# Two attention score maps in one tile of two PSUM banks, the neighbourhood bias added by VectorE, and another order of the mixers' steps

## The chip, the cores and the metric

The kernel runs on one core of a Trainium2 chip. The metric is the time on the device, in microseconds (us), of one execution of the whole program. TensorE is called PE here, VectorE DVE, ScalarE ACT, GpSimd POOL, and SyncE, which issues most of the transfers, SP.

## What is computed

The reference runs 256 latent tokens of width 1024, with 256 context tokens beside them, through two blocks of two layers each. The change touches the first block alone, and of it the four mixers and the projection behind them. Cut to these:

```python
def first_block(...):                       # layers l = 0, 1
    mod = s_c @ ada_w[l] + ada_b[l]         # six vectors; the same for the context
    hx = rms_norm(x, norm1_g[l]) * (1.0 + sc1) + sh1
    y  = token_mixers(hx, hc, ...)          # below
    x  = x + g1 * y
    x  = x + g2 * expert_choice_ffn(...)    # router, 16 experts

def token_mixers(...):
    ya = chunk_spatial_gating(aX, ...)      # gating
    yb = fourier_mix(bX)                    # Fourier
    # C, differential attention: two maps per head
    s = einsum('bqhmd,bkhmd->bhmqk', q, k) * 32 ** -0.5
    a = softmax(s)
    w = a[:, :, 0] - lam * a[:, :, 1];  yc = w @ v
    # D, neighbourhood attention: bias on the local keys, then all keys
    s_loc = q @ k_blk * 64 ** -0.5 + bias
    p = softmax(concat(s_loc, s_ctx));  yd = p @ v
    # merge: every group normed per head of 64, then the output matrix
    y = rms_norm(concat(ya, yb, yc, yd)) * head_scale
    return y @ w_out
```

In layer 0 the context tokens pass the mixers too (4 tiles of 128 tokens, `nt` = 4), in layer 1 only the latent tokens do (`nt` = 2).

## The kernel before, in words

Each layer of the first block goes through the mixers and the projection (`mixers` L621, `project` L604 on), the router, and 16 experts with their weights streamed from HBM. The second block follows and is not touched.

**How the mixers are staged.** The normed input is transposed by PE (`hx` L286 to L301, tiles `pt`). Column blocks of the input matrix give queries, keys and values (products `pj`, three matmuls for each piece since the operands are split in a high and a low part, L316 to L318; the split of a weight tile is L62 on ACT and L63 on DVE). `diff_unit` (L438 to L468) is one unit of C, a tile of 128 queries and one head with its two maps. `na_unit` (L470 to L502) is one unit of D, a tile of queries and two heads. Layer 0 has 16 units of C and 8 of D, layer 1 has 8 and 4. In both, each of the two score maps has a PSUM tile `psc` of one bank. In a unit of D on latent queries (t < 2, four units in each layer) the bias is put into PSUM by a matmul with the identity (L484), the scores are added to it (L485), DVE takes the row maximum (L489) and negates it (L490), ACT takes the exponentials `e` (L494), PE transposes them into the same bank (L426), ACT copies them out as `wT` (L428), PE multiplies with the values into the same bank (L435), and DVE writes the scaled result to `y` (L502):

```python
nc.tensor.matmul(ps[:, 0:256], C.id, bias[:, i], start=True, stop=False, skip_group_check=True)
nc.tensor.matmul(ps[:, :n], self.dqT[r, j, ...], self.dkT[r, j, k0:k0 + n], start=(t >= 2), ...)
...
wT = self.weights_T(M, pss[i], es[i], n)
o = self.pv(pss[i], wT, n, self.dv, t0, h)
```

The bias tile of a unit has one buffer and comes from HBM by SP's queue (L476). Between these steps stand those of the modulation (`pada`, L182, with its own row `ab` loaded by POOL's queue, L171), of the Fourier part (`bz`, F) and of the gating (s).

**Norm and merge.** Each of the four results y0 (gating), y1 (Fourier), y2 (C), y3 (D) is squared on ACT (L558), summed on DVE (L559), scaled (L560), put through ten small DVE operations of an inverse root (L37 to L41) and multiplied on DVE (L366). `merge` (L575 to L588) transposes them on PE (tiles `pty`, one bank, L583), ACT and DVE write them out as `yT` (L587, L588). The first column block of the projection adds the groups up in the order `self.ks`.

**What sets the order.** `ORDER1` is a string for each layer that lists the steps: ck, cq, cv and dk, dq, dv are projections, C and D the attentions, aN stands for N modulation steps, oN for the norm of group N, r for the router. The order of the o entries is also `ks`. A list scheduler then places every instruction on its engine by data dependencies and estimated durations, so the strings give priorities and the final order is the scheduler's.

**PSUM.** The projections have two banks (`acc`), the scores and transposes four (`E.s`, pool `ps`, four buffers of one bank), `m` and `ada` one each.

Of the kernel before, what the change touches and what calls it, by code (L numbers as in the profile page):

```python
# [14 lines left out]
D = 1024  # L15
# [81 lines left out]
def load_consts0(E, pool):  # L97
# [11 lines left out]

ORDER1 = ("ck a3 cv cq C dk a3 a3 a2 dv a3 dq bz F a2 D s a3 o1 o2 a5 r o0 o3",  # L110
          "ck a4 a1 cv cq C dk a2 bz dv a3 dq s a1 F a5 D a6 o1 r o0 o2 o3")

# [91 lines left out]
class G1:  # L204
# [75 lines left out]
    def hx(self, M):  # L280
# [7 lines left out]
        for s in range(2):  # L288
# [3 lines left out]
            for k in range(0, KC, 2):  # L292
                pt = E.s.tile([128, 2, 256], FT, name="pt1", tag="s")
                for j in range(2):
# [144 lines left out]
    def diff_unit(self, M, t, h):  # L439
# [5 lines left out]
        rq = self.rq[:, 8 * t + 2 * h:8 * t + 2 * h + 2]  # L445
        pss, es = [], []
        for i in range(2):
            f = 64 * (h % 2) + 32 * i
            r = slice(f, f + 32)
            ps = E.s.tile([128, 512], FT, name="psc", tag="s")  # L450
            nc.tensor.matmul(ps[:, :n], self.cqT[r, h // 2, 128 * t:128 * t + 128], self.ckT[r, h // 2, k0:k0 + n], start=True, stop=True)  # L451
            pss.append(ps)
        for i in range(2):
            nc.vector.tensor_reduce(mx[:, i:i + 1], pss[i][:, :n], axis=AX.X, op=OP.max)
        nc.vector.scalar_tensor_tensor(mx, mx, -1.0, rq, op0=OP.mult, op1=OP.mult)
# [14 lines left out]
    def na_unit(self, M, t, j):  # L470
# [3 lines left out]
        if t < 2:  # L474
            bias = M.tile([128, 2, 256], FT, name="bias", tag="bias", bufs=1)
            nc.sync.dma_start(bias, E.i["na_bias"][self.l, :, t, 2 * j:2 * j + 2])  # L476
        sm = E.md.tile([128, 2], FT, name="smd", bufs=4)
        mx = E.md.tile([128, 2], FT, name="mxd", bufs=4)
        pss = []
        for i in range(2):  # L480
            r = slice(64 * i, 64 * i + 64)
            ps = E.s.tile([128, 512], FT, name="psc", tag="s")
            if t < 2:
                nc.tensor.matmul(ps[:, 0:256], C.id, bias[:, i], start=True, stop=False, skip_group_check=True)  # L484
            nc.tensor.matmul(ps[:, :n], self.dqT[r, j, 128 * t:128 * t + 128], self.dkT[r, j, k0:k0 + n],  # L485
                             start=(t >= 2), stop=True, skip_group_check=True)
            pss.append(ps)
        for i in range(2):
            nc.vector.tensor_reduce(mx[:, i:i + 1], pss[i][:, :n], axis=AX.X, op=OP.max)  # L489
        nc.vector.tensor_scalar(mx, mx, -1.0, None, op0=OP.mult)  # L490
# [82 lines left out]
    def merge(self):  # L573
# [4 lines left out]

        self.ks = [2 * int(st[1]) + j for st in ORDER1[self.l].split() if st[0] == "o" for j in range(2)]
        for k in self.ks:  # L580
            pt = E.s.tile([128, 512], FT, name="pty", tag="s")
            for t in range(nt):
                nc.tensor.transpose(pt[:, 128 * t:128 * t + 128], self.y[k // 2][:, t, 128 * (k % 2):128 * (k % 2) + 128], C.id)  # L583
            g = self.pc[:, 16 + k:17 + k]
            for s in range(nt // 2):
                p = pt[:, 256 * s:256 * s + 256]
                nc.scalar.activation(yT[2 * s][:, k], p, AF.Copy, scale=g)  # L587
                nc.vector.scalar_tensor_tensor(yT[2 * s + 1][:, k], p, g, yT[2 * s][:, k], op0=OP.mult, op1=OP.subtract)  # L588
# [32 lines left out]
    def mixers(self):  # L621
        E, l, mods = self.E, self.l, self.mods
        pool = E.tc.tile_pool
        with pool(name=f"mix{l}", bufs=1) as M, \
                pool(name=f"ps{l}", bufs=4, space=PSUM) as E.s, pool(name=f"pm{l}", bufs=1, space=PSUM) as E.m, \
                pool(name=f"pd{l}", bufs=1, space=PSUM) as E.ad:
# [1213 lines left out]
```

## Time and profile before

| what | value |
|---|---|
| median of 3 runs | 2824.7 us (2815.96 to 2825.24) |
| the profiled execution | 2826.67 us |
| its span in the trace | 2824.9 us |
| mean granted PE clock | 0.96 |
| busy: PE, weight loads, DVE, ACT, POOL | 2527.0, 1740.5, 1354.1, 818.2, 243.5 us |

By the names of the instructions in the timeline the span falls into these stages: start 0 to 45 us, mixers and projection of layer 0 to 345, router to 375, experts to 860, mixers and projection of layer 1 to 1045, router to 1075, experts to 1545, and the second block to 2825. A window's row gives the busy time of each engine in it, and the granted clock as a share of full speed; a matmul in fp32 appears as several records, whose pipelined ends overlap.

### The profile page before, as it was taken

The numbers are of one execution on the slowest core, as the hardware profiler recorded it, in microseconds if no ns is written. First come the engines' busy times: TensorE is split into PE (matmuls) and PEld (weight loads), VectorE is DVE, ScalarE is ACT, GpSimd is POOL, SyncE is SP. The second block draws the span as 40 slices with busy tenths as digits, with TensorE's granted clock in tenths as the row PEclk, the third lists the DMA queues.
The fourth block names the chain that finished last, engine by engine and source line by source line (L and its number), as shares of the span: only waits on it lengthen the run. The fifth ranks groups of instructions, "written<-read, shape, count | busy, mean of one in ns | idle before, by whom it ended". The sixth has DMA issues, their size and how long they took to land.

```text
span 2824.9 us, 42465 instructions
## 1 busy us (share of the span) xinstructions
PE 2527.0 (89%) x17771; PEld 1740.5 (62%) x17771; DVE 1354.1 (48%) x2663; ACT 818.2 (29%) x1339; POOL 243.5 (9%) x293
## 2 busy tenths in 40 slices
PE   6999989988889997666667999999999999999998
PEld 4776743322227662111114988888997888879996
DVE  4446533232236562001103768456656667556765
ACT  2334311000014430000002434334444433334442
POOL 1000110000000010000000122000202031100200
PEclk9999999999999999888899998999999998999999
DMA  7434469999995568999996421335654431325553
GB/s 292 180 120 147 164 272 421 422 421 421 421 381 181 185 242 360 422 421 421 421 421 264 155 91 53 113 111 175 209 181 138 152 118 46 105 90 194 179 192 121
DMA packets 237459, 665.60 MB, mean 236 GB/s; under 512 B 11572, under 2 KB 165860, under 8 KB 182356
## 3 DMA queue, kind: packets, MB, share of 16 engines
q1 hardware_dynamic: 235428, 657.81, 61.2%
q0 software_dynamic: 1696, 4.59, 0.5%
q8 instruction: 139, 2.28, 0.3%
q14 instruction: 52, 0.43, 0.0%
q10 hardware_dynamic: 144, 0.49, 0.0%
HBM read 661.78 MB, written 1.05 MB: 235 GB/s over the span
## 4 chain that ended last, share of the span: by engine, by line
PE 59%; DMA 24%; issue 9%; DVE 5%; POOL 2%; ACT 1%; SPq 0%; DVEq 0%; ACTq 0%; POOLq 0%
DMA w<-in_exp_w_up 8%; DMA w<-in_exp_w_down 8%; PE acc L84 6%; PE acc L86 6%; DMA w<-in_exp_w_gate 6%; PE acc L85 6%; PE pj L316 3%; PE pj L318 3%; PE pgate L862 3%; PE pj L317 3%; PE pd L862 2%; PE pup L862 2%; PE pada L182 2%; PE psc L435 1%; PE psc L451 1%
## 5 line engine op out<-in xcount | busy, mean ns | idle before, releaser
L63 DVE TENSOR_TENSOR whl<-w,whl 128x1024 fp32r<-128x1024 f32 x376 | 469.2, 1251 | 310.0 <-ACT whl L62 309.4
L62 ACT ACTIVATE whl<-w 128x1024 fp32r<-128x1024 f32 x376 | 396.2, 1058 | 472.3 <-PE acc L86 237.0
L84 PE MATMUL acc<-xh,whl 128*128 128x256 f32 x1664 | 476.5, 286 | 0.5 <-DVE xh L1619 0.5
L86 PE MATMUL acc<-xh,whl 128*128 128x256 f32 x1664 | 471.7, 283 | 0.2
L85 PE MATMUL acc<-xl,whl 128*128 128x256 f32 x1664 | 471.1, 283 | 0.0
L84 PEld LDWEIGHTS acc<-xh,whl 128*128 128x128 f32 x1664 | 316.7, 190 | 11.0 <-issue 6.5
L86 PEld LDWEIGHTS acc<-xh,whl 128*128 128x128 f32 x1664 | 316.4, 190 | 5.6 <-issue 3.6
L85 PEld LDWEIGHTS acc<-xl,whl 128*128 128x128 f32 x1664 | 316.8, 190 | 3.3 <-issue 2.5
L862 PE MATMUL pup<-w,xg 128*64 128x512 f32 (+1 forms) x1024 | 221.4, 662 | 67.9 <-DMA w<-in_exp_w_up 67.9
L862 PE MATMUL pgate<-w,xg 128*64 128x512 f32 (+1 forms) x1016 | 218.5, 648 | 45.8 <-DMA w<-in_exp_w_gate 43.4
L862 PE MATMUL pd<-w,ehT 128*64 128x512 f32 (+1 forms) x1024 | 202.7, 622 | 59.3 <-DMA w<-in_exp_w_down 42.3
L862 PEld LDWEIGHTS pup<-w,xg 128*64 128x64 f32 (+1 forms) x1024 | 52.6, 130 | 228.7 <-DMA w<-in_exp_w_up 149.6
L862 PEld LDWEIGHTS pd<-w,ehT 128*64 128x64 f32 (+1 forms) x1024 | 51.7, 125 | 186.5 <-DMA w<-in_exp_w_down 87.2
L862 PEld LDWEIGHTS pgate<-w,xg 128*64 128x64 f32 (+1 forms) x1016 | 50.9, 127 | 177.7 <-DMA w<-in_exp_w_gate 91.8
L316 PE MATMUL pj<-whl,hT 128*128 128x256 f32 x496 | 144.5, 292 | 6.1 <-ACT hT L300 5.8
L318 PE MATMUL pj<-whl,hT 128*128 128x256 f32 x496 | 143.3, 290 | 0.9 <-DVE hT L301 0.9
L317 PE MATMUL pj<-whl,hT 128*128 128x256 f32 x496 | 142.8, 289 | 0.0
L893 DVE TENSOR_TENSOR od<-pd,g 128x512 f32<-128x512 f32 x24 | 16.6, 691 | 232.0 <-PE pd L862 232.0
L881 DVE SCALAR_TENSOR_TENSOR et<-et,pup 128x512 f32<-128x512 f32 x24 | 16.5, 687 | 224.0 <-PE pup L862 223.8
L316 PEld LDWEIGHTS pj<-whl,hT 128*128 128x128 f32 x496 | 94.5, 191 | 24.7 <-issue 10.9
L317 PEld LDWEIGHTS pj<-whl,hT 128*128 128x128 f32 x496 | 94.5, 191 | 13.1 <-issue 8.9
L318 PEld LDWEIGHTS pj<-whl,hT 128*128 128x128 f32 x496 | 94.5, 191 | 8.5 <-issue 5.7
(607 smaller groups left out, 4158.9 us busy)
## 6 DMA issues: line engine op xcount, KB each, us to landing
w<-in_exp_w_down SPq DMA_DIRECT2D x128, 1024.0 KB, 19.8
w<-in_exp_w_up SPq DMA_DIRECT2D x127, 1024.0 KB, 19.8
w<-in_exp_w_gate SPq DMA_DIRECT2D x125, 1024.0 KB, 19.8
w<-in_w_in SPq DMA_DIRECT2D x82, 1024.0 KB, 5.1
w<-in_ada_w SPq DMA_DIRECT2D x48, 1024.0 KB, 6.4
w<-in_w_ffn_up SPq DMA_DIRECT2D x44, 1024.0 KB, 5.1
w<-in_w_ffn_down SPq DMA_DIRECT2D x22, 1024.0 KB, 4.8
w<-in_w_out SPq DMA_DIRECT2D x16, 1024.0 KB, 5.5
```

The lines of the kernel that those rows point to most:

```text
L62: nc.scalar.activation(h, w, AF.Copy)
L63: (engine or nc.vector).tensor_sub(lo, w, h)
L84: nc.tensor.matmul(ps[:, b], h[:, k], xh[:, k], start=(k == 0), stop=False)
L85: nc.tensor.matmul(ps[:, b], h[:, k], xl[:, k], start=False, stop=False)
L86: nc.tensor.matmul(ps[:, b], lo[:, k], xh[:, k], start=False, stop=(k == KC - 1))
L182: nc.tensor.matmul(self.ps[32 * j:32 * j + 32], self.st[:, k], ws[j], start=(k == 0), stop=(k == KC - 1), skip_group_check=True)
L316: nc.tensor.matmul(ps, xh, wh, start=start, stop=False, skip_group_check=bool(ks))
L317: nc.tensor.matmul(ps, xh, wl, start=False, stop=False, skip_group_check=bool(ks))
L318: nc.tensor.matmul(ps, xl, wh, start=False, stop=stop, skip_group_check=bool(ks))
L435: self.E.nc.tensor.matmul(o, wT[:, 128 * c:128 * c + 128], v[:, t0 + c, 64 * h:64 * h + 64], start=(c == 0), stop=(c == n // 128 - 1))
L451: nc.tensor.matmul(ps[:, :n], self.cqT[r, h // 2, 128 * t:128 * t + 128], self.ckT[r, h // 2, k0:k0 + n], start=True, stop=True)
L862: m = nc.tensor.matmul(ps[64 * h + mw * i:64 * h + mw * i + mw], lhs(kk, i, e), ws[i][k][:, 512 * h:512 * h + 512], start=(kk == 0), stop= ...
```

## The change

It does four things. (1) The two maps of a unit of C, and the two heads of a unit of D, get one tile `psc` of two banks in place of two tiles of one, and one reduction takes both row maxima. (2) The bias of D is no longer put into PSUM by matmuls with the identity; DVE adds it in place to the scores, one instruction of 128 partitions by 2 by 256 for each of the four latent units of a layer, and the bias tile is loaded by POOL's queue instead of SP's. (3) The transposes of `hx` and of `merge` use tiles of two banks, which hold four and two pieces, and the pool `E.s` has two buffers of two banks in place of four of one. (4) `ORDER1` puts D right behind C and its projections, ahead of Fourier and gating, spreads the modulation steps anew, and turns the o entries from 1, 2, 0, 3 (layer 0) and 1, 0, 2, 3 (layer 1) into 2, 3, 1, 0 in both.

```diff
@@ -107,8 +107,9 @@
 CAP = 32
 GELU_C = math.sqrt(2.0 / math.pi)
 
-ORDER1 = ("ck a3 cv cq C dk a3 a3 a2 dv a3 dq bz F a2 D s a3 o1 o2 a5 r o0 o3",
-          "ck a4 a1 cv cq C dk a2 bz dv a3 dq s a1 F a5 D a6 o1 r o0 o2 o3")
+
+ORDER1 = ("ck a3 cv cq C dk dv dq D a3 a3 a3 bz F a3 o2 s o3 o1 a4 a5 r o0",
+          "ck a4 a1 cv cq C dk dv dq D a2 bz a3 F a5 s a6 a1 o2 o3 o1 r o0")
 
 EARLY = ((("exp_w_gate", 1), ("exp_w_up", 1)), (("exp_w_gate", 1),))
 RINGS = ("xxxwswsws", "xxxxxwswtswts")
@@ -290,7 +291,9 @@
             for t in range(2 * s, 2 * s + 2):
                 nc.vector.tensor_scalar(xn[t], self.xt(t), r[:, t:t + 1], None, op0=OP.mult)
             for k in range(0, KC, 2):
-                pt = E.s.tile([128, 2, 256], FT, name="pt1", tag="s")
+                if k % 4 == 0:
+                    pt4 = E.s.tile([128, 4, 256], FT, name="pt1", tag="s")
+                pt = pt4[:, k % 4:k % 4 + 2]
                 for j in range(2):
                     for t in range(2):
                         nc.tensor.transpose(pt[:, j, 128 * t:128 * t + 128], xn[2 * s + t][:, 128 * (k + j):128 * (k + j) + 128], C.id)
@@ -443,15 +446,15 @@
         sm = E.md.tile([128, 2], FT, name="sme", bufs=4)
         mx = E.md.tile([128, 2], FT, name="mx", bufs=4)
         rq = self.rq[:, 8 * t + 2 * h:8 * t + 2 * h + 2]
-        pss, es = [], []
+        es = []
+
+        ps = E.s.tile([128, 2, 512], FT, name="psc", tag="s")
+        pss = [ps[:, i] for i in range(2)]
         for i in range(2):
             f = 64 * (h % 2) + 32 * i
             r = slice(f, f + 32)
-            ps = E.s.tile([128, 512], FT, name="psc", tag="s")
-            nc.tensor.matmul(ps[:, :n], self.cqT[r, h // 2, 128 * t:128 * t + 128], self.ckT[r, h // 2, k0:k0 + n], start=True, stop=True)
-            pss.append(ps)
-        for i in range(2):
-            nc.vector.tensor_reduce(mx[:, i:i + 1], pss[i][:, :n], axis=AX.X, op=OP.max)
+            nc.tensor.matmul(ps[:, i, :n], self.cqT[r, h // 2, 128 * t:128 * t + 128], self.ckT[r, h // 2, k0:k0 + n], start=True, stop=True)
+        nc.vector.tensor_reduce(mx, ps[:, :, :n], axis=AX.X, op=OP.max)
         nc.vector.scalar_tensor_tensor(mx, mx, -1.0, rq, op0=OP.mult, op1=OP.mult)
         for i in range(2):
             e = M.tile([128, 512], FT, name="e", tag="e2", bufs=6)
@@ -473,20 +476,18 @@
         k0, n, t0 = (0, 512, 0) if t < 2 else (256, 256, 2)
         if t < 2:
             bias = M.tile([128, 2, 256], FT, name="bias", tag="bias", bufs=1)
-            nc.sync.dma_start(bias, E.i["na_bias"][self.l, :, t, 2 * j:2 * j + 2])
+            nc.gpsimd.dma_start(bias, E.i["na_bias"][self.l, :, t, 2 * j:2 * j + 2])
         sm = E.md.tile([128, 2], FT, name="smd", bufs=4)
         mx = E.md.tile([128, 2], FT, name="mxd", bufs=4)
-        pss = []
+
+        ps = E.s.tile([128, 2, 512], FT, name="psc", tag="s")
+        pss = [ps[:, i] for i in range(2)]
         for i in range(2):
             r = slice(64 * i, 64 * i + 64)
-            ps = E.s.tile([128, 512], FT, name="psc", tag="s")
-            if t < 2:
-                nc.tensor.matmul(ps[:, 0:256], C.id, bias[:, i], start=True, stop=False, skip_group_check=True)
-            nc.tensor.matmul(ps[:, :n], self.dqT[r, j, 128 * t:128 * t + 128], self.dkT[r, j, k0:k0 + n],
-                             start=(t >= 2), stop=True, skip_group_check=True)
-            pss.append(ps)
-        for i in range(2):
-            nc.vector.tensor_reduce(mx[:, i:i + 1], pss[i][:, :n], axis=AX.X, op=OP.max)
+            nc.tensor.matmul(ps[:, i, :n], self.dqT[r, j, 128 * t:128 * t + 128], self.dkT[r, j, k0:k0 + n], start=True, stop=True)
+        if t < 2:
+            nc.vector.tensor_add(ps[:, :, 0:256], ps[:, :, 0:256], bias)
+        nc.vector.tensor_reduce(mx, ps[:, :, :n], axis=AX.X, op=OP.max)
         nc.vector.tensor_scalar(mx, mx, -1.0, None, op0=OP.mult)
         es = []
         for i in range(2):
@@ -577,8 +578,10 @@
         self.yT = yT = [E.st.tile([128, 8, 256], FR, name=f"yT{j}", tag="st") for j in range(nt)]
 
         self.ks = [2 * int(st[1]) + j for st in ORDER1[self.l].split() if st[0] == "o" for j in range(2)]
-        for k in self.ks:
-            pt = E.s.tile([128, 512], FT, name="pty", tag="s")
+        for n, k in enumerate(self.ks):
+            if n % 2 == 0:
+                pt2 = E.s.tile([128, 2, 512], FT, name="pty", tag="s")
+            pt = pt2[:, n % 2]
             for t in range(nt):
                 nc.tensor.transpose(pt[:, 128 * t:128 * t + 128], self.y[k // 2][:, t, 128 * (k % 2):128 * (k % 2) + 128], C.id)
             g = self.pc[:, 16 + k:17 + k]
@@ -622,7 +625,7 @@
         E, l, mods = self.E, self.l, self.mods
         pool = E.tc.tile_pool
         with pool(name=f"mix{l}", bufs=1) as M, \
-                pool(name=f"ps{l}", bufs=4, space=PSUM) as E.s, pool(name=f"pm{l}", bufs=1, space=PSUM) as E.m, \
+                pool(name=f"ps{l}", bufs=2, space=PSUM) as E.s, pool(name=f"pm{l}", bufs=1, space=PSUM) as E.m, \
                 pool(name=f"pd{l}", bufs=1, space=PSUM) as E.ad:
             if l == 0:
                 mods.start()
```

PE's order at the end of D in layer 0, before: `psc_N<-dkT,dqT` is a head's scores, `psc_N<-cst0_98,e_N` the transposes of its exponentials, `psc_N<-dv,wT` its product with the values; numbers tell tiles apart.

```order
L485 MATMUL psc_2058<-dkT_1337,dqT_1675 128x256
L485 MATMUL psc_2060<-dkT_1337,dqT_1675 128x256
L435 MATMUL psc_2029<-dv_1417,wT_2044 128x64 x2
L435 MATMUL psc_2031<-dv_1417,wT_2051 128x64 x2
L678 MATMUL pb_2522<-rw_2515,mt1_1391 2x16 x8
L485 MATMUL psc_2087<-dkT_1337,dqT_1675 128x256
L485 MATMUL psc_2089<-dkT_1337,dqT_1675 128x256
L426 MATMUL psc_2058<-cst0_98,e_2065 128x128 x2
L426 MATMUL psc_2060<-cst0_98,e_2067 128x128 x2
L435 MATMUL psc_2058<-dv_1417,wT_2073 128x64 x2
L435 MATMUL psc_2060<-dv_1417,wT_2080 128x64 x2
```

The same place with the change, from unit 3 of 8 on (line numbers are those of the changed kernel, `psc_N` is now the tile of a unit):

```order
L429 MATMUL psc_1655<-cst0_98,e_1663 128x128 x4
L438 MATMUL psc_1655<-dv_1318,wT_1682 128x64 x4
L487 MATMUL psc_1729<-dkT_1301,dqT_1558 128x256 x2
L429 MATMUL psc_1693<-cst0_98,e_1699 128x128 x4
L438 MATMUL psc_1693<-dv_1318,wT_1709 128x64 x4
L429 MATMUL psc_1693<-cst0_98,e_1701 128x128 x4
L438 MATMUL psc_1693<-dv_1318,wT_1720 128x64 x4
L429 MATMUL psc_1729<-cst0_98,e_1734 128x128 x2
L487 MATMUL psc_1756<-dkT_1301,dqT_1558 128x256 x2
L438 MATMUL psc_1729<-dv_1318,wT_1742 128x64 x2
L429 MATMUL psc_1729<-cst0_98,e_1736 128x128 x2
L438 MATMUL psc_1729<-dv_1318,wT_1749 128x64 x2
```

Before, the two heads of a unit stand side by side (both transposes, both products), each in its own tile, with the next unit's scores between. Now a head's transposes come only after the product of the head before it in the same tile, and nothing but a unit's scores stands between them.

DVE's order behind the last two results of D in layer 0, before (`y3` is D's result, L588 writes other groups' transposes out):

```order
L502 TENSOR_SCALAR y3_331<-psc_2116,rcd_2127 128x64
L502 TENSOR_SCALAR y3_331<-psc_2118,rcd_2127 128x64
L559 TENSOR_REDUCE gsy3_2556<-gsq_2558 128x16
L588 SCALAR_TENSOR_TENSOR yT1_2576<-pty_2597,pc1_141,yT0_2575 128x256
L560 TENSOR_SCALAR gsy3_2556<-gsy3_2556 128x16
L588 SCALAR_TENSOR_TENSOR yT1_2576<-pty_2606,pc1_141,yT0_2575 128x256
L588 SCALAR_TENSOR_TENSOR yT1_2576<-pty_2615,pc1_141,yT0_2575 128x256
L37 TENSOR_SCALAR rsy_y3_2562<-gsy3_2556 128x16
L588 SCALAR_TENSOR_TENSOR yT1_2576<-pty_2624,pc1_141,yT0_2575 128x256
L588 SCALAR_TENSOR_TENSOR yT3_2578<-pty_2597,pc1_141,yT2_2577 128x256
```

The same place with the change, and further down the multiplications of the three groups that are still open:

```order
L503 TENSOR_SCALAR y3_327<-psc_1810,rcd_1819 128x64
L591 SCALAR_TENSOR_TENSOR yT3_2522<-pty_2523,pc1_141,yT2_2521 128x256
L560 TENSOR_REDUCE gsy3_2362<-gsq_2364 128x16
L560 TENSOR_REDUCE gsy1_2381<-gsq_2383 128x16
L561 TENSOR_SCALAR gsy3_2362<-gsy3_2362 128x16
L560 TENSOR_REDUCE gsy0_2499<-gsq_2501 128x16
L561 TENSOR_SCALAR gsy1_2381<-gsy1_2381 128x16
L37 TENSOR_SCALAR rsy_y3_2368<-gsy3_2362 128x16
L561 TENSOR_SCALAR gsy0_2499<-gsy0_2499 128x16
L37 TENSOR_SCALAR rsy_y1_2387<-gsy1_2381 128x16
L39 SCALAR_TENSOR_TENSOR rst_y3_2369<-rsy_y3_2368 128x16
L37 TENSOR_SCALAR rsy_y0_2505<-gsy0_2499 128x16
```

Before, only y3's norm was still to be done there, between the evacuations of the other groups. Now the norms of y3, y1 and y0 run there step by step side by side, and their three multiplications stand together at the end.

PE's order at the merge of layer 0, before (the last of 72 products `pj` of y1, y2 and y0, then y3's transposes):

```order
L318 MATMUL pj_2683<-whl_2676,yT3_2578 128x256
L316 MATMUL pj_2683<-whl_2676,yT2_2577 128x256
L317 MATMUL pj_2683<-whl_2676,yT2_2577 128x256
L318 MATMUL pj_2683<-whl_2676,yT3_2578 128x256
L583 MATMUL pty_2633<-cst0_98,y3_331 128x128 x4
L583 MATMUL pty_2642<-cst0_98,y3_331 128x128 x4
```

With the change (D's last product with the values stands five rows above, and of the 12 products `pj` of y2 behind it the last eight stand here):

```order
L320 MATMUL pj_2622<-whl_2619,yT0_2519 128x256
L321 MATMUL pj_2622<-whl_2619,yT1_2520 128x256
L319 MATMUL pj_2623<-whl_2619,yT2_2521 128x256
L320 MATMUL pj_2623<-whl_2619,yT2_2521 128x256
L321 MATMUL pj_2623<-whl_2619,yT3_2522 128x256
L319 MATMUL pj_2623<-whl_2619,yT2_2521 128x256
L320 MATMUL pj_2623<-whl_2619,yT2_2521 128x256
L321 MATMUL pj_2623<-whl_2619,yT3_2522 128x256
L586 MATMUL pty_2540<-cst0_98,y3_327 128x128 x4
L586 MATMUL pty_2557<-cst0_98,y1_325 128x128 x4
L319 MATMUL pj_2622<-whl_2619,yT0_2519 128x256
```

The transposes of y3, and behind them those of y1, now stand behind 12 products instead of 72, and all products that follow need them. In layer 1 they stand directly behind D's last product, where 54 products came first before.

## Rows read from the trace of the kernel before

**Rows 1.** Busy time by window: length, PE, PEld, DVE, ACT, POOL, PEclk, DMA share, GB/s; mixers' stages.

```profile
45.00:345.00 300.00, 297.64 (x2063) 229.32 (x2060) 169.54 (x435) 114.15 (x241) 14.74 (x23) 0.99 0.45 159
...
860.00:1045.00 185.00, 180.82 (x1272) 141.98 (x1271) 112.96 (x287) 77.82 (x142) 5.43 (x11) 1.00 0.51 180
```

**Rows 2.** Bias matmuls: group by form (busy, mean ns, idle before), whole run.

```profile
L484 PE MATMUL psc<-bias,cst 128*128 128x256 f32 x32 | 10.2, 401 | 0.0
```

**Rows 3.** Timeline, two places in D, PE alone: start, length, line, operation.

```profile
248.07 0.28 PE L318 MATMUL pj<-whl,hT 128*128 128x256 f32 x1
...
248.20 0.60 PE L426 MATMUL psc<-cst,e 128*128 128x128 f32 x4
...
248.63 0.60 PE L484 MATMUL psc<-bias,cst 128*128 128x256 f32 x2
...
249.06 0.60 PE L426 MATMUL psc<-cst,e 128*128 128x128 f32 x4
...
1003.93 0.60 PE L484 MATMUL psc<-bias,cst 128*128 128x256 f32 x2
1004.46 1.12 PE L485 MATMUL psc<-dkT,dqT 64*128 64x512 f32 x2
```

**Rows 4.** Busy time by window, near the start of C in layer 0.

```profile
112.00:117.00 5.00, 4.33 (x19) 2.10 (x20) 4.33 (x8) 3.52 (x7) 0.00 (x0) 1.00 0.90 358
117.00:124.00 7.00, 7.00 (x26) 3.71 (x26) 2.68 (x7) 1.63 (x4) 0.00 (x0) 0.51 0.58 190
```

**Rows 5.** Timeline, one copy between transposes and product in D.

```profile
267.47 0.38 PE L426 MATMUL psc<-cst,e 128*128 128x128 f32 x2
...
267.95 0.38 ACT L428 ACTIVATE wT<-psc 128x256 f32<-128x256 f32 x1 [0.27 <-PE psc L426]
268.41 0.97 PEld L435 LDWEIGHTS psc<-dv,wT 128*128 128x128 f32 x8 [0.33 <-ACT wT L428]
```

**Rows 6.** Groups by form between 225 and 300 us (D of layer 0).

```profile
L428 ACT ACTIVATE wT<-psc 128x512 f32<-128x512 f32 x8 | 4.6, 594 | 3.9 <-PE psc L426 3.9
L502 DVE TENSOR_SCALAR y<-psc,rcd 128x64 f32<-128x64 f32 x16 | 4.5, 281 | 3.3 <-PE psc L435 3.1
```

**Rows 7.** Group by form up to 260 us: a DVE operation with two operands, one in PSUM.

```profile
L528 DVE TENSOR_TENSOR gq<-gq,pj 128x512 f32<-128x512 f32 x4 | 2.6, 680 | 0.1
```

**Rows 8.** Busy time by window: D in layer 0, then the merges of layers 0 and 1.

```profile
225.00:300.00 75.00, 73.31 (x495) 54.57 (x494) 54.91 (x166) 37.22 (x87) 1.64 (x3) 1.00 0.36 122
...
285.00:297.00 12.00, 10.55 (x75) 9.11 (x75) 7.45 (x21) 4.06 (x9) 0.00 (x0) 1.00 0.45 152
1020.00:1030.00 10.00, 9.39 (x61) 6.99 (x59) 6.69 (x14) 5.00 (x7) 0.00 (x0) 1.00 0.86 297
```

**Rows 9.** Timeline of DVE and ACT, y3's norm in layer 0.

```profile
279.79 0.61 DVE L502 TENSOR_SCALAR y<-psc,rcd 128x64 f32<-128x64 f32 x2
280.44 1.06 ACT L558 ACTIVATE gsq<-y 128x1024 f32<-128x1024 f32 x1 [1.10 <-DVE y L502]
281.53 1.22 DVE L559 TENSOR_REDUCE gsy<-gsq 128x16 f32<-128x1024 f32 x1 [1.12 <-ACT gsq L558]
...
287.57 1.23 DVE L366 TENSOR_TENSOR y<-y,gry 128x1024 f32<-128x1024 f32 x1
```

**Rows 10.** Timeline of DVE, layer 1, small operations of several norms side by side.

```profile
1008.60 0.24 DVE L41 SCALAR_TENSOR_TENSOR rsy_y<-rst_y,rsy_y 128x8 f32<-128x8 f32 x2
...
1008.83 0.23 DVE L39 SCALAR_TENSOR_TENSOR rst_y<-rsy_y 128x8 f32<-128x8 f32 x2
```

**Rows 11.** Groups by form between 980 and 1030 us (norms of layer 1).

```profile
L559 DVE TENSOR_REDUCE gsy<-gsq 128x8 f32<-128x512 f32 x4 | 2.7, 681 | 0.3 <-ACT gsq L558 0.3
L558 ACT ACTIVATE gsq<-y 128x512 f32<-128x512 f32 x4 | 2.4, 622 | 0.5 <-DVE y L520 0.5
```

**Rows 12.** Transfers issued between 30 and 350 us: count, KB each, us to landing.

```profile
bias<-in_na_bias SPq DMA_DIRECT2D x3, 256.0 KB, 3.7
ab<-in_ada_b POOLq DMA_DIRECT2D x8, 8.0 KB, 4.2
```

## The prediction

> **What bounds the kernel now.** I read the windows by stage first. In the two mixer stages PE is busy 297.64 of 300 and 180.82 of 185 us at a granted clock of 0.99 and 1.00, DVE 57 to 61%, ACT 38 to 42% [rows 1]. So there a microsecond of PE work removed is a microsecond won, and one in which PE waits is one lost; work on DVE or ACT costs only where PE waits for it. The experts and the second block run the same instructions as before and only shift. Then I read the groups by form for durations, the timeline for the spacing of instructions, and the order of the changed kernel for who stands behind whom. A measurement of this kernel can tell a change of about 0.5%, 14.1 us of the median 2824.7. The sum is made against the profiled execution, 2826.67 us, which stands 2.0 above that median.
>
> **The bias matmuls go.** There are 16 (two layers, four latent units, two heads), and the 32 records are two for each [rows 2]. On PE the next instruction starts 0.43 us after one in layer 0 (248.63 to 249.06) and 0.53 after one in layer 1 (1003.93 to 1004.46) [rows 3]; the group's whole busy time is 10.2 us [rows 2]. Ends: 16 x 0.43 = 6.9 and 10.2. I take 16 x 0.53: **-8.5**. The adds on DVE replace them: eight, each of 512 elements a partition, for which the nearest row is an operation on the same amount with one operand in PSUM, 680 ns [rows 7]. They lie between a unit's scores and its maximum. Where other PE work stands there they are hidden; otherwise each unit's chain grows by 0.7. The fused maximum reads in one instruction what two read before, so at worst it costs what they did. Both are hidden while PE has two units in flight; without that cover the adds cost 8 x 0.68 = 5.4, which goes into the upper end.
>
> **The start of C in layer 0.** Between 112 and 117 us PE is busy 4.33 of 5, and its work is spread thin (19 records); from 117 to 124 the granted clock is 0.51, its lower level, after which it is back [rows 4]. At half the clock 7 us do the work of 3.6: 3.4 lost, and some 2 us of gaps ahead. The order of the changed kernel has 26 to 30 products of projections between each two steps of C there, where before there were two. I take both as gone: **-5.4**, with 0 as the other end, since the same wait for weights may come back elsewhere.
>
> **The tail of D.** The order shows that a head's transposes now stand behind the product of the head before it in the same tile, so I take it that PE waits for the whole tile: head 1's transposes for DVE's read of head 0, and the next unit but one for the read of head 1. The price of a hand-off: two transposes start at 267.47, and four issue in 0.43 (248.20 to 248.63 [rows 3]), so two are out after 0.22; the product starts at 268.41 [rows 5]. That is 0.72 us without PE work for a copy of 0.38, and 0.94 for the copy of 594 ns [rows 6]. A read by DVE (281 ns [rows 6]) with the same 0.34 of hand-off is 0.62. Before, the other head's work lay in both. In layer 0 no filler is left from the second half of unit 3 on: unit 3 pays 1.4 (one copy, one read, less some of the next scores), unit 4 two long copies and a read, 2.5; units 5 to 7 two short copies and a read, 2.06, less 0.3 of scores between, 3 x 1.76 = 5.3; unit 8 has products of y2 in it and pays about 1. That is 10.2, less the 1.7 that PE idles there now (75.00 less 73.31 [rows 8]): +8.5. Layer 1 has full-size units alone and its last two have little filler: 2.5 + 1.6, less about 0.9 of now: +3.2. Together **+11.7**. Ends: 0, if the waits are per head after all, and 17 with the adds.
>
> **The merge.** Now y3 comes last in the sum and 72 products of the other groups hide its norm. With the change y3 is second, behind 12 products, and DVE does three norms side by side. From D's last product in layer 0: the read 0.3, y3's square 1.06 after a start of 0.1, three sums of 1.22 [rows 9], about 28 small operations at the 0.08 at which those of several norms follow each other (1008.60 to 1008.83 is three [rows 10]) 2.2, the multiplication 1.23 [rows 9], some 0.25 of hand-offs: 8.8. Twelve products at 0.13 (248.07 to 248.20 [rows 3]) take 1.5 off it. Behind it y1's transposes, which stand ahead of all further products, wait for one more multiplication and themselves take 0.6: +1.8. So 9.1, less the 1.45 idle there now [rows 8]: 7.6. In layer 1 the square is 0.62, the sums 0.68 [rows 11] and the multiplication, an estimate from these, 0.7, which makes 6.2, no product in front, and 1.1 behind; less the 0.6 of now [rows 8]: 6.7. Together **+14.3**; at the low end, 5, the squares and sums of y1 and y0 are long done and only y3's own chain with its small operations counts.
>
> **The clock.** After a wait like the merge's PE may come back at the lower level. I price one such fall like that at 117 us: **+3.4**, ends 0 and four falls (tail and merge of each layer), 13.6.
>
> **The rest.** The first transposes of `hx` fill a tile of two banks before both evacuations let it go: **+1** (0 to 3). The bias moves to POOL's queue, where small transfers landed after 4.2 us against 3.7 on SP [rows 12]; units of D are 8 to 13 us apart in layer 0, and its one buffer is free early: hidden there, and about 0 to 2 in layer 1. On SP the projection's weights no longer stand behind a bias transfer that waits for its buffer: hidden anyway, PE waits for none of them now.
>
> **Sum.** -8.5 - 5.4 + 11.7 + 14.3 + 3.4 + 1 = +16.5, so 2843.2 against the profiled execution and **2841** against the median.
>
> **The rivals.**
> 1. *The heads do not wait for each other.* The tile has two banks, one for each head, and the first head's copy ran beside the second head's transposes before (transposes at 249.06 while the copy of those at 248.20 was still to come [rows 3]). If waits go by bank the tail costs nothing: 16.5 - 11.7 = +4.8, or 2829.5. Against it speaks the order itself, which would have no reason to alternate. The Trainium skill, page "PSUM — Partial Sum Buffer", in its summary of rules for kernel authors, advises guarding PSUM by bank and reading one bank while a matmul runs into another; by that rule each head would be free of the other. The trace of before agrees for separate tiles; no run here shows it for a shared one.
> 2. *The other side: tail and merge are both hidden.* If the adds' latency is covered, the tiles wait by bank and y3's chain is done early, because D stands ahead of Fourier and gating and their work lies behind it, then only the removed work counts: -8.5 - 5.4 + 1 = -12.9, or 2811.8. It decides at whether Fourier, gating or projection products lie on PE behind D's last unit; by the order 12 in layer 0 and none in layer 1 do, which speaks against it.
> 3. *The clock stays low.* If PE falls to the lower level in the tail and in the merge of both layers, 4 x 3.4 in place of 3.4: +26.7, or 2851.4. For it speaks that a stretch busy 4.33 of 5 was enough for a fall [rows 4]; against it, that the merge now, busy 10.55 of 12, keeps 1.00 [rows 8]. The Trainium skill, page "TensorE: Matmul & The Clock Gate", section "HAM oscillation — how this bites in real kernels", says that idle gaps repeated in a loop bring the clock down each time; by that rule the time would be this rival's, and the trace agrees at 117 us alone.
> 4. *The bias comes late.* If POOL's queue delays it by the whole landing time at a unit of layer 1, about +4 on top: 2845.
>
> **How the numbers follow.** The forecast has 0.45, and its own range, 2832 to 2849, has the bound 2838.8 a little below its middle (0.19 no change, 0.26 slower). Rival 1 has 0.20, all within 0.5%. Rival 2 has 0.15 and lies about the bound 2810.6: 0.10 faster, 0.05 not; it gets the more there since the gain at the start of C could be larger. Rival 3 has 0.15 and rival 4 0.05, both slower. That makes faster 0.10, same 0.19 + 0.20 + 0.05 = 0.44, slower 0.26 + 0.15 + 0.05 = 0.46. The range runs from 2814 to 2855: it leaves out most of rival 2 and the upper part of rival 3.
>
> **What would show it.** Right: PE rows of L487 without a bias matmul before them; the granted clock near 1 from 105 to 125 us; PE busy clearly below 90% over the last units of D, with the idle time ahead of the transposes put down to DVE's `y` and that ahead of the products to ACT's `wT`; a gap of 6 to 9 us on PE ahead of y3's transposes in layer 0 and of 5 to 7 in layer 1, ended by DVE. Wrong: transposes of head 1 that start beside the copy of head 0 (rival 1), merges without a gap (rival 2), clocks of 0.5 in both tails (rival 3), the add waiting for a transfer (rival 4).

## The result, and the profile after

The changed kernel takes 2847.33 us (median of 5 runs, 2841.14 to 2854.45) against 2824.7: a ratio of 1.009 (95% interval 1.0074 to 1.0106), 22.6 us slower. The forecast of 2841 lies 6 us under it, and its range holds it. The profiled execution is the fastest of the five, 2841.14 us with a span of 2839.4, so the stages below add up to 14.5 us and not to 22.6.

| place in the timeline, us | before | after |
|---|---|---|
| first scores of C, layer 0 | 95.3 | 96.9 |
| end of D's last product, layer 0 | 280.1 | 291.9 |
| first product of the router, layer 0 | 336.1 | 357.7 |
| end of the experts, layer 0 | 834.5 | 858.0 |
| end of D's last product, layer 1 | 1013.4 | 1027.3 |
| first product of the router, layer 1 | 1045.4 | 1065.4 |
| end | 2824.9 | 2839.4 |

Layer 0 loses 21.6 us up to its router. Layer 1, from the end of the experts to its router, takes 207.4 us in place of 210.9: it gains 3.5. The second block, which the change doesn't touch, is 4.3 shorter in this execution (1293.3 from its first product to the end in place of 1297.6; 1289.3 to 1299.8 in the profiles of the experiments), so that much is scatter.

The PE timeline of the changed kernel at the end of D in layer 0 and at the merge (start, length, operation, and in brackets the idle time ahead and what ended it):

```profile
256.42 1.12 PE L429 MATMUL psc<-cst,e 128*128 128x128 f32 x4 [2.42 <-DVE y L503]
258.27 1.97 PE L438 MATMUL psc<-dv,wT 128*128 128x64 f32 x8 [0.73 <-ACT wT L431]
...
270.27 1.23 PE L487 MATMUL psc<-dkT,dqT 64*128 64x256 f32 x4
271.43 1.11 PE L438 MATMUL psc<-dv,wT 128*128 128x64 f32 x4
272.98 0.69 PE L429 MATMUL psc<-cst,e 128*128 128x128 f32 x2 [0.44 <-DVE y L503]
274.14 1.11 PE L438 MATMUL psc<-dv,wT 128*128 128x64 f32 x4 [0.47 <-ACT wT L431]
275.05 0.69 PE L429 MATMUL psc<-cst,e 128*128 128x128 f32 x2
275.67 1.23 PE L487 MATMUL psc<-dkT,dqT 64*128 64x256 f32 x4
...
300.97 2.31 PE L586 MATMUL pty<-cst,y 128*128 128x128 f32 x8 [7.09 <-DVE gry L41]
```

This is the alternation that the order promised: a head's transposes wait for DVE's read of the head before (0.44), its product for ACT's copy (0.47 to 0.73), and a unit of 256 keys takes 5.40 us (270.27 to 275.67). Then PE stands still for 7.09 us until y3's norm is done (the row names L41, a step of the norms that run beside it); in layer 1 for 6.14. The windows over the same stretches (length, busy time of PE, PEld, DVE, ACT, POOL, granted clock, DMA share, GB/s):

```profile
139.00:150.00 11.00, 10.50 (x44) 4.20 (x44) 4.80 (x9) 3.83 (x10) 1.65 (x3) 0.55 0.94 374
...
257.00:291.00 34.00, 28.20 (x113) 20.93 (x112) 9.38 (x28) 10.89 (x33) 0.00 (x0) 0.51 0.11 34
294.00:300.90 6.90, 0.00 (x0) 0.00 (x0) 6.90 (x38) 1.40 (x2) 0.00 (x0) 0.73 0.00 1
300.90:307.00 6.10, 5.76 (x25) 5.13 (x26) 4.41 (x9) 2.37 (x5) 0.00 (x0) 0.50 0.00 0
1008.00:1040.00 32.00, 23.39 (x157) 18.57 (x158) 19.50 (x83) 12.25 (x25) 0.54 (x1) 0.85 0.05 15
```

In the 34 us from 257 on PE is busy 28.20 at 0.51, its lower level of 1.2 GHz, where the kernel before had 1.00 throughout D [rows 8]. At full clock the same work would take half of it, so by this estimate the clock alone costs some 14 us there. And the fall of [rows 4] is not gone, it comes at 140 us: just ahead of it PE runs out of work behind a weight transfer. Two rows of the PE timeline that end in a DMA:

```profile
139.50 1.38 PE L183 MATMUL pada<-w,cst 128*32 128x512 f32 x8 [1.51 <-DMA w<-in_ada_w]
...
235.86 1.94 PE L183 MATMUL pada<-w,cst 128*32 128x512 f32 x8 [2.50 <-DMA w<-in_ada_w]
```

One thing went the other way. The score groups by form over the whole run (busy, mean ns, idle before), before:

```profile
L451 PE MATMUL psc<-ckT,cqT 32*128 32x512 f32 x64 | 30.1, 655 | 0.0
L485 PE MATMUL psc<-dkT,dqT 64*128 64x512 f32 x32 | 18.0, 641 | 0.0
L451 PE MATMUL psc<-ckT,cqT 32*128 32x256 f32 x32 | 11.1, 426 | 0.0
```

and after:

```profile
L456 PE MATMUL psc<-ckT,cqT 32*128 32x512 f32 x64 | 16.8, 671 | 0.0
L487 PE MATMUL psc<-dkT,dqT 64*128 64x512 f32 x32 | 10.0, 703 | 0.2 <-DVE y L503 0.2
L456 PE MATMUL psc<-ckT,cqT 32*128 32x256 f32 x32 | 5.6, 426 | 0.4 <-DVE y L471 0.4
```

The same number of records, each about as long as before (10% longer at most), and yet they cover little more than half the time: 18.8 us less for C (41.2 to 22.4) and 8.0 for the large units of D. The prediction has no term for that.

What this comes to is read from the windows of the two whole stages, from 45 us or the end of the experts to the router, before:

```profile
45.00:336.10 291.10, 288.74 (x2019) 224.72 (x2015) 162.08 (x416) 111.60 (x235) 10.95 (x21) 0.99 0.45 159
834.50:1045.40 210.90, 200.41 (x1369) 151.21 (x1370) 135.52 (x342) 89.38 (x161) 5.43 (x11) 0.97 0.54 192
```

and after:

```profile
45.00:357.70 312.70, 287.57 (x1999) 228.01 (x2000) 162.63 (x396) 114.27 (x235) 12.65 (x24) 0.91 0.42 147
858.00:1065.40 207.40, 186.08 (x1352) 148.15 (x1352) 136.83 (x334) 89.58 (x161) 8.55 (x15) 0.94 0.54 196
```

PE's idle time (length less busy time) rises by 33.6 us, from 12.9 to 46.5. The stretches at the lower level hold 17 us of its busy time before and 66 after; half of that is lost, so the clock takes some 24 us more. What is left of the busy time, the work counted at full clock, falls by some 40 us. But for rounding these three make up the 18.1 us that both stages lose together.

### The profile page after: what moved, and what is told of

It reads as the page before. It is cut to its first block, busy times and chain, and to the rows that moved or that the text cites. A ratio compares the mean times of both kernels' runs of the same rounds, so it can differ in the third digit from the quotient of the medians.

```text
span 2839.4 us, 42392 instructions
## 1 busy us (share of the span) xinstructions
PE 2505.3 (88%) x17739; PEld 1736.0 (61%) x17739; DVE 1357.5 (48%) x2635; ACT 821.7 (29%) x1339; POOL 243.8 (9%) x301
## 4 chain that ended last, share of the span: by engine, by line
PE 64%; DMA 26%; DVE 7%; ACT 1%; issue 1%; POOL 0%; SPq 0%; DVEq 0%; ACTq 0%; POOLq 0%
DMA w<-in_exp_w_down 9%; DMA w<-in_exp_w_up 8%; PE acc L84 8%; PE acc L86 8%; PE acc L85 8%; DMA w<-in_exp_w_gate 6%; PE pj L321 3%; PE pj L320 3%; PE pj L319 3%; PE pgate L865 3%; PE pd L865 2%; PE pup L865 2%; PE dn L1543 2%; PE dn L1542 2%; PE dn L1544 2%
## 5 line engine op out<-in xcount | busy, mean ns | idle before, releaser
L84 PEld LDWEIGHTS acc<-xh,whl 128*128 128x128 f32 x1664 | 316.9, 190 | 10.7 <-issue 6.5
L865 PE MATMUL pd<-w,ehT 128*64 128x512 f32 (+1 forms) x1024 | 209.0, 643 | 56.7 <-DMA w<-in_exp_w_down 39.6
```

Source lines behind the costliest of these rows:

```text
L84: nc.tensor.matmul(ps[:, b], h[:, k], xh[:, k], start=(k == 0), stop=False)
L865: m = nc.tensor.matmul(ps[64 * h + mw * i:64 * h + mw * i + mw], lhs(kk, i, e), ws[i][k][:, 512 * h:512 * h + 512], start=(kk == 0), stop= ...
```

## The experiments

Ratios are against the kernel before, run beside each on the same chip.

| experiment | median us | ratio, 95% interval |
|---|---|---|
| e1 one-bank tiles, the rest changed | 2826.34 | 1.0012 (1.0001 to 1.0022) |
| e2 changed, old order strings | 2831.53 | 1.0034 (1.0022 to 1.0046) |
| e3 before, bias by DVE alone | 2825.41 | 1.0013 (0.9998 to 1.0028) |
| e4 changed, y3 added up last | 2844.63 | 1.0078 (1.0058 to 1.0098) |
| e5 changed, heads side by side | 2826.15 | 1.0008 (0.9997 to 1.0019) |
| e6 one-bank, bias by DVE, y3 last | 2822.32 | 0.9996 (0.9985 to 1.0008) |
| e7 before, new order, y3 last | 2829.51 | 1.0028 (1.0015 to 1.0041) |
| e8 before, two-bank tiles alone | 2846.25 | 1.0078 (1.0062 to 1.0094) |
| e9 as e5, y3 last | 2815.11 | 0.9969 (0.9959 to 0.9979) |
| e10 as e9, hx in one-bank buffers | 2817.32 | 0.9976 (0.9967 to 0.9985) |
| e11 as e5, old order strings | 2831.20 | 1.0032 (1.0020 to 1.0045) |
| e12 as e9, C's two scores kept apart | 2855.67 | 1.0115 (1.0097 to 1.0133) |

**e1, the tiles undone.** The tiles of `hx` and `merge` and the pool's four buffers of one bank are back too.

```diff
-        ps = E.s.tile([128, 2, 512], FT, name="psc", tag="s")
+            ps = E.s.tile([128, 512], FT, name="psc", tag="s")
...
-            nc.vector.tensor_add(ps[:, :, 0:256], ps[:, :, 0:256], bias)
+                nc.vector.tensor_add(ps[:, 0:256], ps[:, 0:256], bias[:, i])
```

> The changed kernel with each map and head in a one-bank tile of its own again (reductions apart, the add on VectorE in two halves); new order of steps, bias by VectorE and by POOL's queue stay. Theory 'the shared tile costs': the alternation of heads and the half clock in the tail of D go, some 12 us of stalls and some 10 of clock over both layers, while the merge with y3 second keeps its 7 us wait: 2827 to 2832 us. Rival 'the order of the steps costs': no change against the changed kernel, 2840 to 2850. Granted clock in D of layer 0 near 1 by the first, 0.5 to 0.7 by the second.

Measured 2826.34, by the first theory and a little under it. D in layer 0 runs at 0.97 and is busy 59.48 of 61 us. What is left is the merge, a PE row of this kernel:

```profile
285.90 3.38 PE L582 MATMUL pty<-cst,y 128*128 128x128 f32 x16 [6.91 <-DVE gry L41]
```

So the wait for y3's norm comes with the order strings, whatever the tiles.

**e2, the strings undone,** all else changed; in layer 0:

```diff
-ck a3 cv cq C dk dv dq D a3 a3 a3 bz F a3 o2 s o3 o1 a4 a5 r o0
+ck a3 cv cq C dk a3 a3 a2 dv a3 dq bz F a2 D s a3 o1 o2 a5 r o0 o3
```

> The changed kernel with the order strings of before; two-bank tiles and bias by VectorE stay. Theory 'the shared tile costs': the last units of D alternate head by head at half clock as in the changed kernel, and only the merge's wait goes (y3 is last again behind the others' products): 2830 to 2838. Rival 'the order costs': back to before less the bias matmuls, about 2816.

2831.53, in the first theory's range: the tail alternates (clock 0.72 and 0.50 in the tens from 260 and 270 us), the wait at the merge is gone.

**e3, the bias alone.**

```diff
-                nc.tensor.matmul(ps[:, 0:256], C.id, bias[:, i], start=True, stop=False, skip_group_check=True)
...
+                nc.vector.tensor_add(ps[:, 0:256], ps[:, 0:256], bias[:, i])
```

> The kernel before with the bias added by VectorE in two halves instead of 16 identity matmuls; tiles, order and SP's queue as before. If the matmuls were pure PE time: 8.5 us less, about 2816. Rival 'the add lengthens a chain that PE waits for': 8 units by 0.8 us back, about 2823, with more PE idle in the last units of D.

2825.41: no gain that can be told from none, so the 8.5 us of the first theory are not there. Windows of layer 1 show where a part of them may have gone:

```profile
985.00:990.00 5.00, 5.00 (x6) 1.17 (x4) 2.23 (x4) 1.10 (x4) 0.00 (x0) 0.51 0.68 220
1000.00:1004.00 4.00, 1.78 (x16) 1.59 (x15) 4.00 (x15) 0.71 (x2) 0.00 (x0) 0.95 0.00 0
1004.00:1012.00 8.00, 7.51 (x48) 7.12 (x49) 6.36 (x45) 3.83 (x9) 0.00 (x0) 0.50 0.02 3
```

Without the matmuls PE waits there, and after a wait its clock is at the lower level, where it had kept 1.00 before [rows 1]. That execution took 2820.03 us, though, close to the lowest of this kernel's runs, and they spread over 15 us, so the place of the loss is likely and not settled.

**e4, y3 last.** In both strings the entry o3 moves to the end; in layer 0:

```diff
-bz F a3 o2 s o3 o1 a4 a5 r o0
+bz F a3 o2 s o1 a4 a5 r o0 o3
```

> The changed kernel with the o entry of y3 put last in both strings, so that the first projection block adds y3 up last; all else as changed. Theory 'the merge waits for y3's norm': the idle stretch of 7 us in layer 0 and 5 to 6 in layer 1 ahead of y3's transposes shrinks to 1 to 2, and the clock fall behind it goes: 2830 to 2836. Rival 'the three norms on VectorE are late whatever the order': 2843 or more.

2844.63, the rival's number, but not for its reason. From D's last product to the router layer 0 takes 59.3 us in place of 65.8 and layer 1 31.6 in place of 38.1: the 13 us are there. D itself is longer, 75.4 for 72.6 and 49.7 for 38.7, which is 13.8. A window of this kernel:

```profile
1005.00:1037.00 32.00, 28.06 (x133) 22.80 (x134) 18.08 (x70) 10.25 (x24) 0.54 (x1) 0.57 0.08 25
```

In layer 1's tail the clock is at 0.57 here, and in the same window of the changed kernel it was at 0.85: what the merge gave, the alternating tail took. Why its clock fell for longer here, no run shows.

**e5, heads side by side in the same tiles.**

```diff
         for i in range(2):
-            h = 2 * j + i
-            wT = self.weights_T(M, pss[i], es[i], n)
-            o = self.pv(pss[i], wT, n, self.dv, t0, h)
+            for c in range(n // 128):
+                nc.tensor.transpose(pss[i][:, 128 * c:128 * c + 128], es[i][:, 128 * c:128 * c + 128], C.id)
...
+        for i in range(2):
+            nc.scalar.activation(wTs[i][:, :n], pss[i][:, :n], AF.Copy)
+        os_ = [self.pv(pss[i], wTs[i], n, self.dv, t0, 2 * j + i) for i in range(2)]
```

> The changed kernel with a unit of D written head beside head in its two-bank tile: both heads' transposes, then both copies, both products, both results. Same tiles, same instructions, same strings. Theory 'the alternation of heads within one tile costs, by whole-tile waits': a unit pays one copy hand-off instead of two and the next unit's scores lie in it, the granted clock in D of layer 0 stays above 0.9, D of layer 0 falls from 72.6 to 58 to 62 us: 2828 to 2835. Rival 'tiles of two banks cost as such, two units in flight are too few': 2842 or more.

2826.15, 21 us under the changed kernel with the same tiles and strings. PE rows of one unit:

```profile
255.50 0.66 PE L501 MATMUL psc<-cst,e 128*128 128x128 f32 x4
256.96 1.50 PE L438 MATMUL psc<-dv,wT 128*128 128x64 f32 x8 [0.81 <-ACT wT L504]
258.25 1.06 PE L501 MATMUL psc<-cst,e 128*128 128x128 f32 x4
259.24 1.23 PE L487 MATMUL psc<-dkT,dqT 64*128 64x256 f32 x4
...
263.10 1.22 PE L487 MATMUL psc<-dkT,dqT 64*128 64x256 f32 x4 [0.73 <-DVE rcd L498]
```

One wait for the copies in a unit, and 3.9 us from scores to scores (259.24 to 263.10) in place of 5.40, still at the lower clock. D of layer 0 takes 55.4 us, less than the 58 to 62 expected, but its clock is 0.87 and does not stay above 0.9. The tile of two banks is not the cost; the alternation in it, with the waits and the clock that it brings, is. Nor is the tile a gain yet: e5 is no faster than e1, where PE is idle for 26.4 us in the two stages and here for 38.8.

**e6 and e7, one-bank tiles with y3 last**, with the bias by DVE and POOL's queue (e6, that is e1 with the strings of e4) and by matmuls (e7, the kernel before with these strings). From e7 to e6:

```diff
-            nc.sync.dma_start(bias, E.i["na_bias"][self.l, :, t, 2 * j:2 * j + 2])
+            nc.gpsimd.dma_start(bias, E.i["na_bias"][self.l, :, t, 2 * j:2 * j + 2])
...
-                nc.tensor.matmul(ps[:, 0:256], C.id, bias[:, i], start=True, stop=False, skip_group_check=True)
...
+                nc.vector.tensor_add(ps[:, 0:256], ps[:, 0:256], bias[:, i])
```

> One-bank tiles and bias by VectorE as in the first experiment, new order, and the o entry of y3 last. In that experiment projection and merge were 6.6 us (layer 0) and 7.0 (layer 1) longer than in the kernel before. Theory 'that is the wait for y3's norm': both come back and the time is 2812 to 2816, below the kernel before. Rival 'what the merge gains, the tail of D loses again through the clock', as with two-bank tiles: 2823 to 2828.

> The kernel before with the new order strings, y3's o entry last, and nothing else: bias still by identity matmuls, one-bank tiles. Against the sixth experiment it differs by the bias alone. If the 16 matmuls are pure PE time: 8 us more than that one. If they are worth nothing because PE waits there anyway and its clock falls without them: the same time within 3 us.

2822.32 and 2829.51: here the matmuls cost 7.2 us, near the 8.5. e7 stands 0.28% above the kernel before, so with tiles of one bank the new order does not pay by itself. e6 misses its theory's 2812 to 2816. Layer 0 gets its 5.7 us at the merge back, layer 1 not (40.3 from D to the router, 39.0 in e1): there gating comes late, with its products behind D's last on PE, and y0 stands ahead of y3 in the sum.

**e8, the two-bank tiles alone,** with the bias by matmuls and the old strings:

```diff
-            ps = E.s.tile([128, 512], FT, name="psc", tag="s")
+        ps = E.s.tile([128, 2, 512], FT, name="psc", tag="s")
...
-                nc.tensor.matmul(ps[:, 0:256], C.id, bias[:, i], start=True, stop=False, skip_group_check=True)
+                nc.tensor.matmul(ps[:, i, 0:256], C.id, bias[:, i], start=True, stop=False, skip_group_check=True)
```

> The kernel before with the two-bank tiles alone (scores, hx, merge; one reduction for two maps); bias by identity matmuls on SP's queue and the order strings as before. Theory 'the shared tile costs in D': the last units of D alternate, 2830 to 2838, as the second experiment plus what the bias matmuls are worth (0 to 8 us). Rival 'the tile is free and the add on VectorE is what costs in the second experiment': 2822 to 2825.

2846.25, above both theories: the alternation shows in the same rows (0.44 and 0.47), and the clock between 250 and 295 us is 0.66. Against e2 the bias by matmuls costs 14.7 us here. In part that is because the second of them also stands between the two heads' scores in a two-bank tile: the large scores of D cover 19.9 us, and 10.0 in e2.

**e9, e10 and e11, what is left.** e9 is e5 with the strings of e4; e10 opens four one-bank buffers for `hx` ahead of the score pool; e11 is e5 with the old strings.

```diff
-                if k % 4 == 0:
-                    pt4 = E.s.tile([128, 4, 256], FT, name="pt1", tag="s")
-                pt = pt4[:, k % 4:k % 4 + 2]
+                pt = P.tile([128, 2, 256], FT, name="pt1", tag="h")
```

> The fifth experiment (heads side by side in the two-bank tile) with y3's o entry last. In that one merge and projection were 11.3 us (layer 0) and 7.2 (layer 1) longer than before. Theory 'that is the wait for y3's norm': 13 us come back, 2812 to 2816, under the kernel before. Rival 'the gain is lost to the clock in the tail', as in the fourth experiment, which got 13 us at the merge and 3 at the end: 2822 or more.

> The ninth with hx transposing into four one-bank buffers of its own, whose banks the score tiles take over afterwards. With two-bank tiles the first scores of C come at 96.9 to 99.6 us, with one-bank tiles at 92.3 to 95.3. If that is the wait for a tile's evacuations: C starts by 94 us and some 3 to 5 us come off the ninth's time over both layers. Rival 'PE has other work there, it is only shifted': same time as the ninth.

> The fifth with the order strings of before. Theory 'with heads side by side only the merge's wait is left of the new order's cost': 2812 to 2818, as the ninth. Rival 'the early attentions help where the tail is cured': 4 us or more above the ninth.

e9 takes 2815.11 us, 0.31% under the kernel before (interval 0.21 to 0.41%): that is in its theory's range. With heads side by side the merge's gain stays (D to router 59.7 and 33.3 us, 67.3 and 39.2 in e5). The tail is not cured of the low clock, as a window of e9 shows:

```profile
251.00:282.00 31.00, 28.47 (x137) 23.44 (x136) 16.05 (x56) 13.15 (x38) 1.67 (x3) 0.51 0.18 58
```

In e10 C starts at 93.6 us in place of 96.3, as expected, and nothing of it is left at the end: only shifted. e11 takes 2831.20, its rival: with heads side by side the new strings with y3 last are worth 16 us. e11 is also no better than e2, so under the old strings putting the heads side by side is worth nothing. Its clock over D of layer 0 is 0.80 where e2 has 0.86, so a part may have gone there; why, no run tells.

**e12, the scores kept apart.**

```diff
+            if i:
+                nc.tensor.matmul(ps[:, 1, 0:32], C.id, C.id[:, 0:32], start=True, stop=True)
             nc.tensor.matmul(ps[:, i, :n], self.cqT[r, h // 2, 128 * t:128 * t + 128], ...)
```

> The ninth experiment with one small matmul between the score matmuls of a C unit's two maps: the identity by its first 32 columns, 24 in all, written where the second map's scores go and overwritten by them. In every two-bank kernel the two maps' scores stand back to back on PE and the four records take 1.06 us; in every one-bank kernel other work stands between and two records take that long. Theory 'back to back on different rows of the array they run side by side, which is the gain of the two-bank tile': time from the score records to the next instruction goes from 12.8 and 7.4 us (layers 0 and 1) to about 24 and 13.7, the kernel gets 15 to 22 us slower than the ninth, 2830 to 2837. Rival 'the shorter records are bookkeeping of the trace': only the added matmuls count, 2 to 5 us, 2817 to 2820.

The PE timeline of e9 and then of e12, one unit of C each:

```profile
111.26 1.13 PE L456 MATMUL psc<-ckT,cqT 32*128 32x512 f32 x4
```

```profile
114.47 1.12 PE L458 MATMUL psc<-ckT,cqT 32*128 32x512 f32 x2
115.53 0.41 PE L457 MATMUL psc<-cst 128*128 128x32 f32 x2
115.86 1.12 PE L458 MATMUL psc<-ckT,cqT 32*128 32x512 f32 x2
```

Four records in 1.13 us side by side, 1.12 for each two apart. From score records to the next instruction layer 0 goes from 12.8 to 25.8 us and layer 1 from 7.4 to 15.8, as the theory said and its rival did not. The median, 2855.67, is 41 us over e9 and so more than the 15 to 22. Its profiled execution, 2836.51, is its fastest run by 10 us and stands 17.5 over e9's span; the other runs' mean clock is lower (0.948 to 0.956, against 0.960), and why it is lower is open. The added matmul also writes where the second scores go, so e12 alone does not tell whether the rows that it takes or the place that it writes parts the two; rows of the kernel before, in the last section, speak for the former.

## Why the prediction came out right, and where it did not

**Bias matmuls, -8.5.** About right where tiles and order stay the same (7.2, e6 against e7). It is not a fixed price: 14.7 with two-bank tiles (e2 against e8), none that can be told in the kernel before (e3).

**Start of C, -5.4.** Wrong: nothing was gained, and its other end, 0, was the better one. The same fall came 20 us later behind a wait for modulation weights, 0.55 at 139 to 150 us, and lasted longer. The prediction had named that end.

**Tail of D, +11.7.** The mechanism is shown by e5 against the changed kernel and by the rows: waits go by whole tile, two hand-offs a unit. The size fits too: PE's idle time within D rises from 0.2 to 10.7 us in layer 0 and from 0.7 to 4.4 in layer 1, and less the 2.50 for weights that makes 11.6. Rival 1, waits by bank, is out: in the tail the transposes of a second head wait for DVE's read in the first head's bank. Rivals 2 and 4 are out as well: both merges have their gap, and no wait for the bias's transfer shows in the trace.

**Merge, +14.3.** Right, and a little high: 7.09 and 6.14 us of standstill ended by DVE's norm, idle time behind D that rises by 6.2 and 5.5 where 7.6 and 6.7 were forecast, and 13.0 that go away with y3 last (e4). The further wait for y1 in layer 0, 1.8 in the forecast, did not come: its transposes follow y3's in one row (300.97, eight records).

**Clock, +3.4.** This is the term that was mis-sized: about 14 us in layer 0's tail alone, by 28.20 busy at 0.51, the price that only its upper end, 13.6 for all four falls, came near; with the merges and two short stretches it is some 22. Each fall was priced like the one at 117 us, and the tail's lasted some five times as long, 34 us. Rival 3, at 0.15, had the mechanism for layer 0; in layer 1 the clock over D was 0.96. The Trainium skill, page "TensorE: Matmul & The Clock Gate", section "HAM oscillation — how this bites in real kernels", says that idle gaps repeated in a loop bring the clock down each time. The trace agrees only in part: the clock falls to 0.51 over a tail whose gaps are 0.44 to 2.42 us, but these are waits for DVE and ACT where the page's loop waits for transfers, and it falls once and stays down.

**What was not in the sum.** The two-bank tile puts two score matmuls next to each other, and on different rows of the array they run side by side: 26.8 us less by the rows above. That is most of the 40 us by which PE's work fell, where the sum had the 8.5 of the bias alone. Against it, the sum had 25 us of waits and 33.6 were measured, and its two clock terms cancelled (-3.4 at C, +3.4 behind the waits) where the clock took 24 more. So the total was right by luck: a gain of some 31 us that no term held against 33 us of clock and waits beyond the forecast. By layer it was not right: the forecast for layer 1 was a loss, and layer 1 gained 3.5.

## What to carry to other kernels

A tile that two independent chains share is waited for as one: write the chains through it side by side, all of one step and then all of the next, or give each its own. Price a stall on PE with its clock: short waits in a row doubled the time of all work between them, so a stretch must be kept filled, and a gain elsewhere can be lost there. Look for matmuls with few rows: two on different rows of the array cost the time of one if nothing stands between them, and a shared tile that frees both at once puts them there.

## What the hardware showed that was not expected

Two score matmuls on 32 (C) or 64 (D) rows each, at different rows, take together the time of one when they follow each other: 1.13 us for four records and 1.12 for two (e9, e12). The kernel before shows it too, for D in tiles of one bank: two heads' scores with transposes on all 128 rows between them, and then two in a row:

```profile
262.31 0.70 PE L485 MATMUL psc<-dkT,dqT 64*128 64x256 f32 x2
262.94 0.66 PE L426 MATMUL psc<-cst,e 128*128 128x128 f32 x4
263.52 0.70 PE L485 MATMUL psc<-dkT,dqT 64*128 64x256 f32 x2
...
267.78 0.70 PE L485 MATMUL psc<-dkT,dqT 64*128 64x256 f32 x4
```

So the shared tile is not what lets them run together; it is what puts them next to each other. The Trainium skill, page "TensorE: Matmul & The Clock Gate", section "The mechanism" of its Part 3 on packing small matmuls, says that matmuls on different tiles of the array run concurrently; the trace agrees. It adds that in e12 a matmul on all 128 rows between them ends it, 0.33 us long and costing the unit 1.06 more besides.
